# The eight scatter steps of an expert pair, three of them between the parts of the lin product or all behind it

## The chip, the cores and the metric

One core of a Trainium2 chip runs the whole kernel in one launch. The metric is the device time of one execution in microseconds (us); three executions of the kernel before are given, and one more that was taken by the hardware profiler. Five engines work side by side, each with its own queue: TensorE (PE; its weight loads are listed apart as PEld), VectorE (DVE), ScalarE (ACT), GpSimd (POOL) and SyncE (SP), which issues most transfers.

## The reference

Two layers over 512 latent tokens of 1024 values: a token mixer (a gated DeltaNet in layer 0, a short gated convolution in layer 1), then in each layer a hierarchical mixture of 32 SwiGLU experts, of which each token uses two. The change lies in the mixture, of which this is the core:

```python
def expert_block(args):
    xi, e = args
    return (jax.nn.silu(xi @ w1[e]) * (xi @ w3[e])) @ w2[e]

yb = lax.map(expert_block, (xb, block_e)).reshape(cap, d)
y = jax.ops.segment_sum(yb * buf_w[:, None].astype(yb.dtype), buf_tok, num_segments=t + 1)
```

Each token's row is gathered, goes through its expert, is weighted, and is added back to the token it came from. All values are float32; w1 and w3 of one expert are 1024 x 512 and w2 is 512 x 1024, 2 MiB each.

## The kernel before, in words

The mixture of a layer is `moe(l)` (L1454 and on). It takes the 32 experts two at a time, 16 pairs `p`, each expert with up to 64 rows, so that a pair fills 128 rows: the first 64 columns of the array hold one expert's rows and the last 64 the other's. If an expert of a pair has more than 64 rows, a second block of 128 rows (tiles `hx`, `gx`) goes through the same weights, under checks of the count `n` (`tc.If(n > 64)`, L1626, L1633 and L1642).

The order of the work in a pair is the order of the program text, as the stage is scheduled by hand:

- `gate_up` (L1499): the w1 product. `up` (L1493) runs over k = 0..7 and over the two experts x, 16 matmuls (32 records, as each float32 matmul leaves two); ScalarE takes silu of the result.
- `lin_up` (L1502): the w3 product in the same way; VectorE multiplies it into `g`. I call it the lin product or the w3 product.
- a scatter of the previous pair's result: eight steps (`scatter_parts`, L1550 to L1559), each of two matmuls of a selection matrix with the high and the low part of the result (L1556, L1557), into one of the PSUM banks `pj`, and one add of that bank to the residual `xs` on VectorE (L1558). There are six `pj` banks (`self.banks = {"tr": 2, "pj": 6}`, L434).
- `turn_g` (L1508, L1510) transposes `g`, `turn` (L1479, L1483, L1485) transposes and modulates the rows `hg` of the next pair to `hT`, half on VectorE and half on ScalarE.
- `down` (L1520 and on): the w2 product in two halves, weighed on VectorE (L1526) and split into a high and a low part on ScalarE (L1530) and GpSimd (L1531).

`up` takes a generator `side` and, after the k of a list, lets it do one step. That is how work is put between the parts of a product:

```python
for _ in range(side[1].count(k) if side else 0):
    next(side[0], None)
```

In the kernel before, the lin product of pairs 1 to 14 gets the scatter with the list (1, 3, 5): a step after k = 1, 3 and 5. The other five follow behind the product, after the check for the second block, the gather for pair p + 2 (GpSimd) and `issue` (SyncE).

The weights come through three rings of 2 MiB slots, 3 + 2 + 4 = 9. `next_unit` takes the next weight, `issue` starts the next transfers in a fixed order (w1, w3, w2 of a pair, two transfers each) as slots come free; a transfer waits on SyncE until the slot's last reader on TensorE is done. The pair 15 of a layer is written apart, with a scatter of its own, and pair 0 has no scatter.

Of the kernel before, what the change touches and what calls it, by code (L numbers as in the profile page):

```python
# [34 lines left out]
class Net:  # L35
# [83 lines left out]
    def plan(self):  # L119
# [18 lines left out]
        def moe(l):  # L138
            for p in range(16):
                for n in ("w1", "w3", "w2"):  # L140
                    order.extend((n, l, 2 * p + x) for x in range(2))
        moe(0)
        for g in range(2):
            order.extend(("w_in_b", 3072, u + g, 0) for u in (0, 2, 4))
            if g == 0:
                order.extend(("ada_w", 6144, 4 * b + u, l) for l, b in self.later for u in range(4))
        order.extend(("w_out_b", 1024, u, 0) for u in range(2))
        moe(1)

        self.place = {o: "B" for o in order if o[0] in ("ada_w", "w_in_b") or o[:2] == ("w2", 0) and o[2] > 29}  # L150
# [1303 lines left out]
    def moe(self, l):  # L1454
        tc, nc, I = self.tc, self.nc, self.I
        with ExitStack() as ms:
# [7 lines left out]
            def gather(gi, hg=None, skip=False, of=None):  # L1464

                if hg is None:
                    hg = wk.tile([128, 1024], F32, name="hg", bufs=2)
                of = self.hscr if of is None else of
                nc.gpsimd.indirect_dma_start(out=hg, out_offset=None, in_=of[:, :],
                                             in_offset=bass.IndirectOffsetOnAxis(ap=gi, axis=0),  # L1470
                                             **(dict(bounds_check=of.shape[0] - 1, oob_is_err=False) if skip else {}))
                return hg

            def turn(hg, to=None):

                hT = (wk.tile([128, 1024], F32, name="hT") if to is None else to).rearrange("p (k d) -> p k d", k=8)
                ps = [self.bank("tr") for _ in range(2)]
                for c in range(8):
                    nc.tensor.transpose(ps[c // 4][:, 128 * (c % 4):128 * (c % 4) + 128], hg[:, c::8], self.ident)  # L1479
                for c in range(8):  # L1480
                    q = ps[c // 4][:, 128 * (c % 4):128 * (c % 4) + 128]
                    if c > 3:
                        nc.scalar.activation(hT[:, c], q, AF.Identity, bias=self.m8[:, l, 2, c:c + 1], scale=self.m8[:, l, 0, c:c + 1])  # L1483
                    else:
                        nc.vector.tensor_scalar(hT[:, c], q, self.m8[:, l, 0, c:c + 1], self.m8[:, l, 2, c:c + 1], op0=OP.mult, op1=OP.add)  # L1485
                return hT

            def up(hT, w, side=()):

                ps = self.bank("pj")  # L1490
                for k in range(8):
                    for x in range(2):
                        nc.tensor.matmul(ps[64 * x:64 * x + 64], hT[:, k, 64 * x:64 * x + 64], w[x][:, k], start=(k == 0), stop=(k == 7))  # L1493
                    for _ in range(side[1].count(k) if side else 0):
                        next(side[0], None)
                return ps

            def gate_up(hT, w, g, side=()):
                nc.scalar.activation(g, up(hT, w, side), AF.Silu)  # L1499

            def lin_up(hT, w, g, side=()):
                nc.vector.tensor_tensor(g, up(hT, w, side), g, op=OP.mult)  # L1502

            def turn_g(g, gT=None):

                pg = self.bank("tr")
                for k in range(4):
                    nc.tensor.transpose(pg[:, 128 * k:128 * k + 128], g[:, k::4], self.ident)  # L1508
                gT = wk.tile([128, 4, 128], F32, name="gT") if gT is None else gT[:, :512].rearrange("p (k d) -> p k d", k=4)
                nc.scalar.activation(gT, pg.rearrange("p (k d) -> p k d", k=4), AF.Copy)  # L1510
                return gT

            def down(gT, w, ti, wi, o, y, eng=nc.gpsimd):

                self.sel(o, ti)
                for n in range(2):
                    py = self.bank("pj")
                    for k in range(4):
                        for x in range(2):
                            nc.tensor.matmul(py[64 * x:64 * x + 64], gT[:, k, 64 * x:64 * x + 64], w[x][:, k, 512 * n:512 * n + 512],  # L1520
                                             start=(k == 0), stop=(k == 3))
                    weigh(py, n, wi, y)
                    split(n, o, y, eng)
# [17 lines left out]
            def ident(x1):  # L1541
                for t in range(4):
                    nc.tensor.matmul(x1[t], self.ident, self.xs[:, t, 512:], start=True, stop=False)
                    yield

            def scatter(*a):
                for _ in scatter_parts(*a):
                    pass

            def scatter_parts(yhi, ylo, sel, ns=(0, 1)):  # L1550
                for n in ns:
                    for t in range(4):
                        ps = self.bank("pj")
                        c = slice(512 * n, 512 * n + 512)
                        s = sel[:, 128 * t:128 * t + 128]
                        nc.tensor.matmul(ps, s, yhi[:, c], start=True, stop=False)  # L1556
                        nc.tensor.matmul(ps, s, ylo[:, c], start=False, stop=True)  # L1557
                        nc.vector.tensor_tensor(self.xs[:, t, c], ps, self.xs[:, t, c], op=OP.add)  # L1558
                        yield n, t  # L1559

            def col(t, c):
                return t[:, c:c + 1]
# [3 lines left out]
            def out():  # L1566
                return tuple(wk.tile([128, m], F32R, name=n) for n, m in (("yhi", 1024), ("ylo", 1024), ("sel", 512)))
# [5 lines left out]
            def more(p):  # L1573
                n = count(slice(p, p + 1))
                with tc.If(n > 64):
                    gather(col(self.gxc, 16 + p), hx[p % 2])
                return n
# [37 lines left out]
            hT = turn(hgs.pop(0))  # L1615
# [4 lines left out]
            prev = None  # L1620
            for p in range(15):
                n = ns.pop(p)
                w = self.next_unit(), self.next_unit(1)
                g = wk.tile([128, 512], F32, name="g")
                gate_up(hT, w, g, () if p else (route, range(8)))
                with tc.If(n > 64):  # L1626

                    hTx = turn(hx[p % 2], hx[p % 2])
                    gate_up(hTx, w, gx)
                w = self.next_unit(), self.next_unit(1)  # L1630
                add = scatter_parts(*prev) if prev else iter(())
                lin_up(hT, w, g, (add, (1, 3, 5)))
                with tc.If(n > 64):  # L1633
                    lin_up(hTx, w, gx)
                if p < 14:
                    hgs.append(gather(col(self.gix, p + 2), skip=True))
                    self.issue(self.taken)
                for _ in add:
                    pass
                w = self.next_unit(), self.next_unit(1)  # L1640
                prev = out()
                with tc.If(n > 64):  # L1642
                    down(turn_g(gx, hx[p % 2]), w, col(self.tid, 16 + p), col(self.wsl, 16 + p), prev, gx)
                    scatter(*prev)
                gT = turn_g(g)
                hT = turn(hgs.pop(0))
                if p < 13:
                    ns[p + 2] = more(p + 2)
                prev = out()
                down(gT, w, col(self.tid, p), col(self.wsl, p), prev, g, nc.gpsimd if p < 14 else nc.vector)  # L1650

            n = count(slice(15, 16))
            w = self.next_unit(), self.next_unit(1)
            g = wk.tile([128, 512], F32, name="g")
            add = scatter_parts(*prev, ns=(1, 0))
            gate_up(hT, w, g, (add, (2, 3, 3, 4, 5, 6, 7)))
            w = self.next_unit(), self.next_unit(1)
            x1 = [self.bank("pj") for _ in range(4)]
            add = chain(add, ident(x1))
# [17 lines left out]
            prev = out()  # L1677
# [252 lines left out]
```

## Time and profile before

| what | us |
|---|---|
| median of three executions | 1875.29 |
| lowest and highest | 1871.93, 1875.86 |
| the profiled execution, its own time | 1876.28 |
| span of the profiled execution | 1874.2 |
| layer 0's expert pairs, first w1 product to the last pair's | 622.6 to 1088.1 |
| layer 1's expert pairs, the same | 1363.3 to 1822.1 |

The span runs from the first to the last instruction; the execution's time has 2.1 us around it. TensorE is busy 91% of the span, and its granted clock is 0.964 of full speed in the mean. The transfers move 572 MB, 305 GB/s over the whole span. The shares are means over stages with different limits: what a saved microsecond is worth is read from the two expert stages themselves.

### The profile page before, as it was taken

Reading aid. Unit: us, or ns where it says so; the run is one execution under the profiler, and the core shown is the slowest. Engines: PE = TensorE matmul, PEld = TensorE weight load, DVE = VectorE, ACT = ScalarE, POOL = GpSimd, SP = SyncE. Lnnn points to the kernel's source line nnn. Section 1 sums busy time; section 2 is a strip of 40 time slices with the busy share of each in tenths; the row PEclk is TensorE's granted clock in tenths of the full one; section 3 lists DMA queues with packets and bytes.
Section 4 is the critical chain, followed back from the end, with each engine's and each line's share of the span. In section 5 each row is a group of like instructions: output and inputs, shape, how many; then the busy total and the mean of one; then the engine's idle time right before and its main releaser. Section 6 shows DMA issues by size and latency. Waiting matters only on the chain. (4 is left out here: it accounts for less than half of the span.)

```text
span 1874.2 us, 26554 instructions
## 1 busy us (share of the span) xinstructions
PE 1709.8 (91%) x10229; PEld 977.8 (52%) x10230; DVE 814.8 (43%) x1611; ACT 483.3 (26%) x888; POOL 415.4 (22%) x297
## 2 busy tenths in 40 slices
PE   5999988997988799999999988999799999999997
PEld 4766667776866344434434336688534344344332
DVE  5435877746664332323323237633523233233233
ACT  4465354523223111111111115223211111111112
POOL 1114464635410101111010103343111111110100
PEclk9999989998998899999999998999899999999998
DMA  9569975779835899999998953714589969999993
GB/s 330 192 241 339 293 222 157 173 170 262 244 107 227 345 425 425 427 425 426 426 425 346 404 193 139 279 40 180 226 340 427 425 268 425 426 425 425 426 418 123
DMA packets 154551, 572.33 MB, mean 305 GB/s; under 512 B 55208, under 2 KB 79961, under 8 KB 126214
## 3 DMA queue, kind: packets, MB, share of 16 engines
q1 hardware_dynamic: 148326, 555.26, 77.6%
q0 software_dynamic: 4896, 10.48, 1.5%
q10 hardware_dynamic: 1152, 4.19, 0.5%
q8 instruction: 115, 1.88, 0.4%
q14 instruction: 62, 0.51, 0.1%
HBM read 550.86 MB, written 26.38 MB: 308 GB/s over the span
## 5 line engine op out<-in xcount | busy, mean ns | idle before, releaser
L1493 PE MATMUL pj<-w,hT 128*64 128x512 f32 x2048 | 482.7, 602 | 7.1 <-DMA w<-in_w 2.5
L1558 DVE TENSOR_TENSOR xs<-pj,xs 128x512 f32<-128x512 f32 x264 | 170.5, 687 | 372.9 <-PE pj L1557 369.1
L1493 PEld LDWEIGHTS pj<-w,hT 128*64 128x64 f32 x2048 | 151.4, 137 | 266.1 <-issue 251.3
L1531 POOL TENSOR_TENSOR ylo<-g,yhi 128x512 fp32r<-128x512 f32 x56 | 70.8, 1265 | 653.4 <-ACT yhi L1530 653.4
L1520 PE MATMUL pj<-w,gT 128*64 128x512 f32 x960 | 212.6, 594 | 3.0 <-DVE hT L1485 1.6
L666 POOL TENSOR_TENSOR wlo<-w,whi 128x1024 fp32r<-128x1024 f32 x43 | 106.5, 2479 | 230.2 <-ACT whi L664 228.7
L1520 PEld LDWEIGHTS pj<-w,gT 128*64 128x64 f32 x960 | 78.1, 137 | 116.5 <-issue 108.8
L1526 DVE SCALAR_TENSOR_TENSOR g<-pj,wsl,gate 128x512 f32<-128x512 f32 x64 | 48.0, 751 | 177.7 <-PE pj L1520 164.1
L1556 PE MATMUL pj<-yhi,sel 128*128 128x512 f32 x264 | 117.5, 445 | 4.9 <-PEq L1633 4.2
L1510 ACT ACTIVATE gT<-tr 128x512 f32<-128x512 f32 x32 | 19.1, 598 | 383.5 <-PE tr L1508 383.5
L1556 PEld LDWEIGHTS pj<-yhi,sel 128*128 128x128 f32 x264 | 49.4, 187 | 120.0 <-issue 90.4
L681 PE MATMUL pj<-w,whi 128*128 128x512 f32 x336 | 105.7, 394 | 0.6 <-ACT whi L664 0.6
L1557 PE MATMUL pj<-ylo,sel 128*128 128x512 f32 x264 | 104.3, 395 | 1.3 <-POOL ylo L1531 1.3
L681 PE MATMUL pj<-hhi,wlo 128*128 128x512 f32 x224 | 93.7, 419 | 8.3 <-POOL wlo L666 7.0
L681 PE MATMUL pj<-hhi,whi 128*128 128x512 f32 x224 | 93.4, 417 | 6.4 <-DVE cv L797 5.5
L681 PE MATMUL pj<-hlo,whi 128*128 128x512 f32 x224 | 91.5, 409 | 0.0
L1530 ACT ACTIVATE yhi<-g 128x512 fp32r<-128x512 f32 x62 | 39.2, 632 | 193.3 <-DVE g L1526 193.3
L681 PEld LDWEIGHTS pj<-w,whi 128*128 128x128 f32 x336 | 63.7, 190 | 15.2 <-ACT whi L664 1.0
L664 ACT ACTIVATE whi<-w 128x1024 fp32r<-128x1024 f32 x53 | 55.3, 1054 | 53.9 <-PE pj L681 37.6
L1499 ACT ACTIVATE g<-pj 128x512 f32<-128x512 f32 x32 | 19.1, 598 | 190.5 <-PEq L1626 141.1
L681 PE MATMUL pj<-w,wlo 128*128 128x512 f32 x168 | 66.3, 394 | 0.0
L1483 ACT ACTIVATE hT<-tr,m 128x128 f32<-128x128 f32 x128 | 48.3, 458 | 55.2 <-PE tr L1479 53.5
(613 smaller groups left out, 2692.1 us busy)
## 6 DMA issues: line engine op xcount, KB each, us to landing
w<-in_w SPq DMA_DIRECT2D x188, 2048.0 KB
w<-in_ada_w SPq DMA_DIRECT2D x20, 2048.0 KB
w<-in_w_in_a SPq DMA_DIRECT2D x8, 2048.0 KB
w<-in_w_in_b SPq DMA_DIRECT2D x6, 2048.0 KB
w<-in_ada_w SPq DMA_DIRECT2D x8, 1024.0 KB
w<-in_w SPq DMA_DIRECT2D x8, 1024.0 KB
Y<-R SPq DMA_DIRECT2D x20, 256.0 KB
vp<-vscr SPq DMA_DIRECT2D x18, 256.0 KB
```

Of the source, the lines that this page charges most:

```text
L664: nc.scalar.activation(hi[:, :, :n], w, AF.Copy)
L666: (lo_eng or nc.gpsimd).tensor_tensor(lo[:, :, :n], w, hi[:, :, :n].bitcast(F32), op=OP.subtract)
L681: nc.tensor.matmul(out, n[j][0][:, k], n[j][1][:, k, a:b], start=(i == 0), stop=(i == 23))
L1483: nc.scalar.activation(hT[:, c], q, AF.Identity, bias=self.m8[:, l, 2, c:c + 1], scale=self.m8[:, l, 0, c:c + 1])
L1493: nc.tensor.matmul(ps[64 * x:64 * x + 64], hT[:, k, 64 * x:64 * x + 64], w[x][:, k], start=(k == 0), stop=(k == 7))
L1520: nc.tensor.matmul(py[64 * x:64 * x + 64], gT[:, k, 64 * x:64 * x + 64], w[x][:, k, 512 * n:512 * n + 512], start=(k == 0), stop=(k == 3))
L1526: nc.vector.scalar_tensor_tensor(y, py, wi, self.gate[:, 512 * n:512 * n + 512], op0=OP.mult, op1=OP.mult)
L1530: nc.scalar.activation(o[0][:, c], y, AF.Copy)
L1531: eng.tensor_tensor(o[1][:, c], y, o[0][:, c].bitcast(F32), op=OP.subtract)
L1556: nc.tensor.matmul(ps, s, yhi[:, c], start=True, stop=False)
L1557: nc.tensor.matmul(ps, s, ylo[:, c], start=False, stop=True)
L1558: nc.vector.tensor_tensor(self.xs[:, t, c], ps, self.xs[:, t, c], op=OP.add)
```

## The change

The lin product of pairs 1 to 14 gets no `side` any more, and all eight scatter steps stand where the last five stood.

```diff
                 w = self.next_unit(), self.next_unit(1)
-                add = scatter_parts(*prev) if prev else iter(())
-                lin_up(hT, w, g, (add, (1, 3, 5)))
+                lin_up(hT, w, g)
                 with tc.If(n > 64):
                     lin_up(hTx, w, gx)
                 if p < 14:
                     hgs.append(gather(col(self.gix, p + 2), skip=True))
                     self.issue(self.taken)
-                for _ in add:
-                    pass
+                if prev:
+                    scatter(*prev)
                 w = self.next_unit(), self.next_unit(1)
```

The lines behind it move up by one (L1633 is L1632 in the changed kernel, L1642 is L1641). The first place is TensorE's queue in a pair of layer 0, from the check behind the w1 product; `hx_5990` is the second block's tile, which is passed over when no expert of the pair has more than 64 rows. Before:

```order
L1493 MATMUL pj<-w,hT 64x512 x4
L1556 MATMUL pj<-yhi,sel 128x512
L1557 MATMUL pj<-ylo,sel 128x512
L1493 MATMUL pj<-w,hT 64x512 x4
L1556 MATMUL pj<-yhi,sel 128x512
L1557 MATMUL pj<-ylo,sel 128x512
L1493 MATMUL pj<-w,hT 64x512 x4
L1556 MATMUL pj<-yhi,sel 128x512
L1557 MATMUL pj<-ylo,sel 128x512
L1493 MATMUL pj<-w,hT 64x512 x4
L1633 COMPARE_AND_BRANCH
```

With the change:

```order
L1493 MATMUL pj<-w,hT 64x512 x16
L1632 COMPARE_AND_BRANCH
L1493 MATMUL pj<-w,hx_5990 64x512 x16
L1632 UNCONDITIONAL_BRANCH x2
L1556 MATMUL pj<-yhi,sel 128x512
L1557 MATMUL pj<-ylo,sel 128x512
L1556 MATMUL pj<-yhi,sel 128x512
L1557 MATMUL pj<-ylo,sel 128x512
```

The product's 16 matmuls stand without a break, and behind the check come eight steps (four of their rows are shown), where five stood.

The second place is VectorE's queue at the same point, up to the next pair's `hT` (the branch at L1642 goes past the second block's work). Before:

```order
L1558 TENSOR_TENSOR xs<-pj,xs 128x512 x3
L1502 TENSOR_TENSOR g<-pj,g 128x512
L1633 COMPARE_AND_BRANCH
L1502 TENSOR_TENSOR gx<-pj,gx 128x512
L1633 UNCONDITIONAL_BRANCH x2
L1558 TENSOR_TENSOR xs<-pj,xs 128x512 x5
L1642 COMPARE_AND_BRANCH
```

With the change:

```order
L1502 TENSOR_TENSOR g<-pj,g 128x512
L1632 COMPARE_AND_BRANCH
L1502 TENSOR_TENSOR gx<-pj,gx 128x512
L1632 UNCONDITIONAL_BRANCH x2
L1558 TENSOR_TENSOR xs<-pj,xs 128x512 x8
L1641 COMPARE_AND_BRANCH
```

The three adds that stood ahead of the product's own multiplication (L1502) stand behind it, in a row of eight, ahead of the branch and of `hT`.

The third place is TensorE's queue behind the row of eight, from the branch past the second block to the w2 product, with the semaphores that each waits for (`DVE_49` is VectorE's count); these rows read the same before, but for the line of the branch:

```order
L1641 UNCONDITIONAL_BRANCH [waits PE_49]
L1508 MATMUL tr<-ident,g 128x128 x4
L1479 MATMUL tr<-ident,hg 128x128 [waits DMASW4_49,PE_49,Activation_49]
L1479 MATMUL tr<-ident,hg 128x128 x3
L1479 MATMUL tr<-ident,hg 128x128 [waits Activation_49]
L1479 MATMUL tr<-ident,hg 128x128 x3
L1570 TENSOR_LOAD cnt_5976
L1575 COMPARE_AND_BRANCH
L1575 UNCONDITIONAL_BRANCH x2
L1520 MATMUL pj<-w,gT 64x512 [waits DMAHW4_49,DVE_49]
```

The transposes wait for ScalarE and for the gathered rows; the w2 product's first matmul waits for its weight and for VectorE's count, which by its place in the program stands behind the eight adds and the branch, not behind `hT`.

## Rows read from the trace of the kernel before

**Rows 1.** The page: busy us of the engines, share of the span, instructions.
```profile
PE 1709.8 (91%) x10229; PEld 977.8 (52%) x10230; DVE 814.8 (43%) x1611; ACT 483.3 (26%) x888; POOL 415.4 (22%) x297
```

**Rows 2.** Stretches: us, engines' busy us, granted clock, DMA share, GB/s; two answers.
```profile
636.10:951.60 315.50, 303.03 (x1348) 128.23 (x1344) 95.07 (x168) 43.67 (x88) 39.82 (x34) 1.00 1.01 425
...
1003.00:1031.00 28.00, 26.33 (x124) 12.93 (x122) 12.88 (x23) 4.61 (x9) 3.81 (x3) 1.00 0.68 289
...
1511.00:1535.80 24.80, 23.14 (x110) 12.08 (x110) 12.87 (x23) 4.61 (x9) 3.81 (x3) 1.00 0.44 171
...
1536.80:1800.80 264.00, 256.95 (x1146) 106.20 (x1142) 82.01 (x144) 36.37 (x74) 33.08 (x28) 1.00 1.01 425
...
1376.80:1494.80 118.00, 113.78 (x518) 47.45 (x516) 32.66 (x60) 17.39 (x36) 15.08 (x13) 1.00 1.01 423
```

**Rows 3.** Timeline of TensorE, pair 4 of layer 0: start us, us, instruction.
```profile
738.60 7.09 PE L1493 MATMUL pj<-w,hT 128*64 128x512 f32 x32
...
745.84 1.94 PE L1493 MATMUL pj<-w,hT 128*64 128x512 f32 x8
...
755.53 0.47 PE L1556 MATMUL pj<-yhi,sel 128*128 128x512 f32 x1 [0.16 <-PEq L1633]
...
756.07 0.40 PE L1556 MATMUL pj<-yhi,sel 128*128 128x512 f32 x1
...
757.45 0.39 PE L1556 MATMUL pj<-yhi,sel 128*128 128x512 f32 x1
...
758.21 0.72 PE L1508 MATMUL tr<-ident,g 128*128 128x128 f32 x4
...
760.54 7.09 PE L1520 MATMUL pj<-w,gT 128*64 128x512 f32 x32 [0.20 <-DVE hT L1485]
...
767.42 1.06 PE L1493 MATMUL pj<-w,hT 128*64 128x512 f32 x4
```

**Rows 4.** Timeline of TensorE, layer 0: pair 11, start of pair 12.
```profile
940.62 7.36 PE L1493 MATMUL pj<-w,hT 128*64 128x512 f32 x32
...
948.12 1.04 PE L1493 MATMUL pj<-w,hT 128*64 128x512 f32 x2
...
951.62 3.08 PE L1493 MATMUL pj<-w,hT 128*64 128x512 f32 x6 [2.46 <-DMA w<-in_w]
...
974.68 7.07 PE L1493 MATMUL pj<-w,hT 128*64 128x512 f32 x32
```

**Rows 5.** Waits of TensorE over the whole span: us in total, times, longest.
```profile
PE pj L1493 <- DMA w<-in_w: 2.5, 1, 2.5
```

**Rows 6.** Instructions on tile hx, TensorE: duration in ns, first and last start.
```profile
L1493 PE MATMUL pj<-w,hx x128: 592/592/643, 983.3 to 1510.6; 128*64 128x512 f32 x128
```

**Rows 7.** Timeline of VectorE, pair 4 of layer 0.
```profile
748.48 0.69 DVE L1558 TENSOR_TENSOR xs<-pj,xs 128x512 f32<-128x512 f32 x1 [8.79 <-PE pj L1557]
...
756.33 3.08 DVE L1558 TENSOR_TENSOR xs<-pj,xs 128x512 f32<-128x512 f32 x5
...
759.57 1.37 DVE L1485 TENSOR_SCALAR hT<-tr,m 128x128 f32<-128x128 f32 x4 [0.15 <-DVEq L1642]
...
760.84 0.48 DVE L1698 TENSOR_SCALAR sel<-tok,tid 128x512 fp32r<-128x512 f32 x1
```

**Rows 8.** Timeline: issues of SyncE, and TensorE at layer 1's pair 14.
```profile
635.12 0.82 SPq L215 DMA_DIRECT2D w<-in_w  x2
...
1375.82 0.81 SPq L215 DMA_DIRECT2D w<-in_w  x2
...
1535.82 17.48 SPq L215 DMA_DIRECT2D w<-in_w  x6
...
1800.78 0.65 PE L1493 MATMUL pj<-w,hT 128*64 128x512 f32 x2 [0.16 <-PEq L1626]
```

**Rows 9.** DMA queues: packets, MB, share of 16 engines.
```profile
q0 software_dynamic: 4896, 10.48, 1.5%
```

**Rows 10.** The stretch behind the wait of pair 11, columns as in rows 2.
```profile
951.60:956.00 4.40, 4.38 (x10) 1.27 (x12) 0.13 (x1) 0.00 (x0) 0.00 (x0) 0.61 1.01 419
```

## The prediction

> **What bounds the kernel now.** I read the page first, then the busy time in stretches of the two expert stages, then one pair of experts on TensorE and VectorE, then the few waits on weights. The page has TensorE busy for 1709.8 of 1874.2 us [rows 1]: it is the engine to look at, but not proof that it sets the end, so the transfers have to be laid beside it. From 636.1 to 951.6 us in layer 0, and from 1536.8 to 1800.8 us in layer 1, the DMA share is full (1.01) at 425 GB/s; but one stretch behind the first (1003 to 1031) and one ahead of the second (1511 to 1535.8) have shares of 0.68 and 0.44: there the transfers stood still for want of a free slot [rows 2]. So there are two regimes, and which one a pair is in decides whether TensorE's time counts.
>
> How fast is each? TensorE takes 28.82 us from one pair's w1 product (738.60) to the next (767.42) [rows 3]. The transfers: the first stretch runs from the second w3 transfer of pair 1, issued at 635.12 [rows 8], to the landing of the second w3 of pair 11, which is 61 transfers of 2 MiB in 315.5 us, 5.17 us each and 31.0 us for the six of a pair. TensorE is faster than the transfers by 2.2 us a pair and lives on a lead: nine slots that were filled ahead. In layer 0 the lead runs out at pair 11: its w3 product, begun at 948.12, stands still for 2.46 us for a weight and goes on at 951.62 [rows 4]; that is the one such wait, 2.5 us, of the whole run [rows 5]. Pair 12 is one with more than 64 rows: its second block of rows (tile hx, from 983.3 on) uses weights that are there already, while the transfers run ahead and stop. Such a pair comes once a layer, since 128 records are four up products, two blocks of two [rows 6]; in layer 1 it is pair 4.
>
> **The change, part by part.** In a pair (1 to 14 of each layer) the w3 product had three scatter steps between its parts; now it has none, and all eight steps follow it.
>
> What is removed from the product: with three steps inside, it takes 745.84 to 755.53, 9.69 us. The w1 product, 32 records of the same kind without a break, takes 738.60 to 745.84, 7.24 us, the check behind it included [rows 3]. The product's own cost is taken as the same, so 2.45 us go, 0.82 for each step.
>
> What is added behind it: in the row of five steps that stands there now, the second begins at 756.07 and the fifth at 757.45, 0.46 us apart [rows 3]. Three more are 1.38 us. So TensorE gains 2.45 - 1.38 = 1.07 us a pair: a step costs 0.82 between column halves and 0.46 among its own kind.
>
> What is moved on VectorE: its three adds of 0.69 us each lay in idle time inside the product [rows 7]; now eight stand in a row. In the row of five they take 3.08 us, 0.62 each, slower than TensorE's 0.46, and begin 0.80 us after the row's first matmul (756.33 after 755.53). Eight end at 0.80 + 8 x 0.62 = 5.8 us. Behind them in VectorE's queue stand the first half of the next pair's hT (759.57, 0.15 us behind the last add) and sel [rows 7]. Who waits for that? The down product waits for VectorE's count behind the adds; TensorE comes to it 760.54 - 755.53 = 5.01 us after the row's start [rows 3], with three more steps at 6.4. The adds are over at 5.8, plus 0.15 for the branch: some 0.45 us to spare. hT is needed only at the next w1 product, 6.9 us later. The seventh and eighth step take over the banks of the first and second (six pj banks, of which the w1 and w3 products have let go): they are issued at 2.8 and 3.2 us, those adds end at 1.4 and 2.0. So VectorE's new tail is costed at nothing, under TensorE's row; if that cover went, its price is that of the second rival. The transfer issues and the gather of the same pair keep their order in the queues of SyncE and GpSimd, and the two issues that wait for the w3 product's end come 2.45 us earlier. They add nothing, as more are waiting in a full queue.
>
> What this is worth, stage by stage. In layer 0 pairs 1 to 10 gain nothing: whatever TensorE saves, the second w3 of pair 11 still lands at 951.6, because the queue was full from 636.1 on [rows 2]. From that landing on, nothing waits for a weight [rows 5], so the w3 product of pair 11 and those of 12, 13 and 14 gain in full: 4 x 1.07 = 4.3 us. In layer 1 pairs 1 to 4 run on a lead, as no wait for a weight stands there at all [rows 5]: another 4.3 us. Their lead carries it: from 1376.8, behind the issue of the second w3 of pair 1 at 1375.82 [rows 8], to pair 4's w3 product 118 us later, 423 GB/s moved 49.9 MB [rows 2], and the 19 transfers needed by then are 39.8 MB. At 1535.82, with the extra block done, the transfers start afresh when TensorE frees a slot [rows 8], so they shift with it and the 4.3 us are kept. From there they run full again, and what TensorE can gain is the lead that is left at pair 14, its last w3 product behind them, begun at 1800.78 [rows 8]. In these 264.0 us, 425 GB/s are 112.2 MB; needed by then are 51 transfers, 106.9 MB, and some 3 MB of gathered rows (10.48 MB for 34 gathers in the whole run [rows 9]). The surplus of 2.3 MB is 5.4 us. But the first stretch shows by how much such a count is ahead of the landing: 134.1 MB by the count against 127.9 + 3 MB needed, a good 7 us in 315.5, or 6 us in 264. So the lead at pair 14 lies between 0 (TensorE did not wait there) and 5.4 us; I take 1 us, near the lower end, for the reason of the first stretch. Behind it pair 14's own row gains its 1.07 us.
>
> The sum: 4.3 + 4.3 + 1.0 + 1.1 = 10.7 us. The profiled execution took 1876.28 us, 2.1 more than its span; that becomes 1865.6. The median of the runs shown, 1875.29, lies 1.0 us under the profiled one, so the predicted median is 1864.6 us. With the bounds of the lead, 0 and 5.4 us, it is 1865.6 and 1860.2.
>
> **A price from a page, weighed.** The row shows 425 GB/s in both stretches [rows 2]. The Trainium skill, "DMA: Bandwidth & Descriptors", Specifications, gives some 358 GB/s per core as what the HBM lets through. By that a pair's 12.9 MB would take an estimated 36 us, every pair would wait for weights, and the change would be worth nothing. The row says otherwise, and the sum goes by the row.
>
> **The rivals.** First: no change. The transfers set the end of both stages and every microsecond saved is waited for again. For it: full DMA share in 580 us of the two stages. Against it: the two stretches at 0.68 and 0.44, where the transfers waited for TensorE. It gives 1875.3 us. The 358 GB/s of the Trainium skill, weighed above, are this rival's rule.
>
> Second, on the other side: the row goes at VectorE's pace. If TensorE had to wait for a bank at each step, the row would take 0.80 + 8 x 0.62 + 0.38 = 6.1 us up to the transposes instead of 8 x 0.46 + 0.38 = 4.1, and a pair would be 1.0 us slower than now. It decides from the point where fewer banks are free than adds are outstanding: at the eighth step VectorE has done (3.2 - 0.8) / 0.62, nearly 4, so 4 are outstanding and 4 banks would be too few; six are there. The price: 14 pairs in layer 1, 14.0 us, and 14 in layer 0, of which the 5.2 us that pair 11 lost (34.06 us from 940.62 to 974.68 [rows 4], against 28.82) come back: 22.8 us, 1898 us. Against it: in the row of five TensorE kept its 0.46 although the adds went at 0.62. The Trainium skill, in "Trainium Kernel Development and Optimization", Best Practices, warns that tiling TensorE speeds up the compute and not the emptying of PSUM, which is this rival's rule; the row of five does not bear it out.
>
> Third: TensorE's whole saving counts, as earlier frees let the transfers go faster: 28 x 1.07 = 30.0 us, 1845 us. For it: TensorE's 91% and a single wait. Against it: 31.0 us a pair at full DMA share, against 27.75 us that TensorE would then take.
>
> Fourth, a smaller gain: the clock. In the 4.4 us behind the 2.46 us stall the granted clock was 0.61 in the mean [rows 10], so it lay at the lower of the two levels for most of them; 0.39 of 4.4 us is 1.7 us lost to TensorE. With the change the lead is used up at 31.0 - 27.75 = 3.25 us a pair: what lasted 10 pairs at 2.2 us in layer 0 lasts nearly 7, and in layer 1 some 1 + 8 x 2.2 us at pair 6 last 6. So stalls of some 3 us in a pair come from pair 7 or 8 on, and in layer 1 from 12 on. In pairs that wait anyway this is hidden; at pair 14 of layer 1 it isn't. Then it is 1866.3 us.
>
> **How the numbers follow.** A measurement of this kernel tells some 0.2%, 3.8 us, from no change. The forecast, with the lead's bounds, has 0.56; the clock or another small loss (a gain of 4 to 9 us) 0.24; no change 0.10; all of TensorE's saving 0.04; slower 0.06. The range reaches from 1858, below the lead's upper bound by a run's scatter of 2 us, to 1871 us, a gain of 4: it leaves out the last three cases, 2 in 10. Faster by over 0.2%: 0.56 + 0.24 + 0.04 = 0.84; within: 0.10; slower: 0.06.
>
> **What would show it.** Right: the w3 product takes 7.2 us in one run of 32 records; eight steps 0.46 us apart; the down product 6.4 us after the row's start; a pair of 27.7 us where no weight is waited for; waits on w in layer 0 from pair 7 or 8 on, some 3 us a pair, and in layer 1 from 12 on; the stretch behind 951.6 shorter by 4.3 us. Wrong: steps 0.62 us apart, or the down product later than 6.6 us after the row's start (VectorE's tail is not covered); w waits in layer 1 before pair 11 (the lead was smaller); no w waits at all (the transfers went faster); or the 4.3 us of layer 0 given back in the mixer between the stages.

## The result, and the profile after

The change takes 1865.45 us (median of 5 runs, 1861.91 to 1865.52) against 1874.16 for the kernel before on the same chip: a ratio of 0.9948 with a 95% interval of 0.9934 to 0.9963, or 7 to 12 us less. The profiled execution took 1864.34 us, its span is 1862.3.

The page has TensorE busy for 1692.0 us, 17.8 less than [rows 1]; the span fell by 11.9. The new row of a pair stands in TensorE's timeline, pair 4 of layer 0 (start us, us, engine, line, operation, tiles, shape, records, and the idle time ahead with what ended it):

```profile
740.23 7.09 PE L1493 MATMUL pj<-w,hT 128*64 128x512 f32 x32 [0.16 <-PEq L1626]
...
751.51 0.72 PE L1508 MATMUL tr<-ident,g 128*128 128x128 f32 x4
...
753.83 7.09 PE L1520 MATMUL pj<-w,gT 128*64 128x512 f32 x32 [0.20 <-DVE hT L1485]
```

The w3 product is one run of 32 records, 740.23 to 747.47 where the first of eight scatter steps begins; it took 9.69 us in [rows 3] and takes 7.24. The steps begin at 747.47, 748.01, 748.47 and so on to 750.74, 0.46 us apart. From one w1 product to the next (733.03 to 760.72) a pair takes 27.69 us, before 28.82. VectorE, same pair:

```profile
748.27 4.87 DVE L1558 TENSOR_TENSOR xs<-pj,xs 128x512 f32<-128x512 f32 x8
753.29 1.37 DVE L1485 TENSOR_SCALAR hT<-tr,m 128x128 f32<-128x128 f32 x4 [0.15 <-DVEq L1641]
```

The eight adds end at 753.14, `hT` begins 0.15 us later, and the w2 product 0.54 us after that. Behind the transposes (751.51) it begins 2.32 us later, as in [rows 3] (758.21 to 760.54): VectorE's longer tail holds nobody up. The bracket of the w2 row names `hT` as what ended its wait in both traces, and the idle time there is 0.20 us in both; which of VectorE's instructions the count stands for, the trace does not tell.

What the pairs wait for, in the stretch of layer 0's pairs and then of layer 1's (TensorE's waits: us in total, times, longest):

```profile
PE pj L1493 <- DMA w<-in_w: 8.3, 5, 2.5
...
PE pj L1493 <- DMA w<-in_w: 4.4, 2, 2.8
```

Before there was one such wait [rows 5]. Now the w3 products of pairs 7 to 11 of layer 0 wait, and these pairs last 29.8, 30.4, 30.6, 30.1 and 33.9 us instead of 27.7; so do pairs 12 and 13 of layer 1 (30.2 and 34.2). TensorE, layer 1's pair 13 and the start of 14:

```profile
1748.81 7.07 PE L1493 MATMUL pj<-w,hT 128*64 128x512 f32 x32
1756.02 1.04 PE L1493 MATMUL pj<-w,hT 128*64 128x512 f32 x2
1759.89 9.96 PE L1493 MATMUL pj<-w,hT 128*64 128x512 f32 x30 [2.83 <-DMA w<-in_w]
1783.03 7.04 PE L1493 MATMUL pj<-w,hT 128*64 128x512 f32 x32
```

Where the 11.9 us of the span come from, by the starts of the w1 products in both timelines (us):

| stretch | before | after | gain |
|---|---|---|---|
| ahead of the experts of layer 0 | 622.58 | 619.75 | 2.83 |
| layer 0, pair 0 to the start of pair 15 | 465.54 | 461.38 | 4.16 |
| pair 15 and the mixer of layer 1 | 275.17 | 276.39 | -1.22 |
| layer 1, pairs 0 to 3 | 115.98 | 112.68 | 3.30 |
| layer 1, pair 4 with its second block | 56.36 | 55.26 | 1.10 |
| layer 1, pairs 5 to 13 | 257.96 | 257.57 | 0.39 |
| layer 1, pair 14 | 28.53 | 27.42 | 1.11 |
| pair 15 and the end | 52.08 | 51.85 | 0.23 |

The stretches with the change in them gain 10.1 us. The first row is scatter: up to there the program is the same, and over the ten profiled executions in which it is (the two above and eight of the experiments) layer 0's pair 0 starts between 618.8 and 624.5 us. So profiles are compared by stretch below, not by span.

### The profile page after: what moved, and what is told of

Same layout as the page of the kernel before. It is cut to its first block, busy times and chain, and to the rows that moved or that the text cites. A ratio compares the mean times of both kernels' runs of the same rounds, so it can differ in the third digit from the quotient of the medians.

```text
span 1862.3 us, 26581 instructions
## 1 busy us (share of the span) xinstructions
PE 1692.0 (91%) x10229; PEld 1002.6 (54%) x10230; DVE 808.3 (43%) x1611; ACT 482.4 (26%) x888; POOL 414.9 (22%) x297
## 5 line engine op out<-in xcount | busy, mean ns | idle before, releaser
L1493 PE MATMUL pj<-w,hT 128*64 128x512 f32 x2048 | 474.2, 602 | 17.5 <-DMA w<-in_w 12.8
L1493 PEld LDWEIGHTS pj<-w,hT 128*64 128x64 f32 x2048 | 167.7, 138 | 295.5 <-issue 262.5
L1502 DVE TENSOR_TENSOR g<-pj,g 128x512 f32<-128x512 f32 x32 | 22.1, 692 | 429.0 <-PEq L1632 386.7
L1558 DVE TENSOR_TENSOR xs<-pj,xs 128x512 f32<-128x512 f32 x264 | 162.5, 681 | 19.2 <-PE pj L1557 15.5
L1556 PE MATMUL pj<-yhi,sel 128*128 128x512 f32 x264 | 108.0, 409 | 4.6 <-DVE g L1526 0.4
```

## The experiments

The theory: a step costs 0.46 us among its own kind and 0.36 more where it breaks a product; the change takes three breaks from every pair, and the saving counts where transfers do not set the pace: pairs 11 to 14 of layer 0, pairs 1 to 4 and 14 of layer 1, and about 1 us of lead in pairs 5 to 13 there. Rivals: all 28 pairs count, or others do; the steps, not the breaks, cost the time; the transfers do not limit.

**The change in the pairs called hidden, and in the others.** Two kernels: the old list where `p` is not in `BARE`, the new order where it is. The first has the pairs below in `BARE`, the second pairs 11 to 14 of layer 0 and 1 to 4 and 14 of layer 1.

```diff
+BARE = {0: range(1, 11), 1: range(5, 14)}
-                lin_up(hT, w, g, (add, (1, 3, 5)))
+                at = () if p in BARE[l] else (1, 3, 5)
+                lin_up(hT, w, g, (add, at))
```

> The change in 19 pairs alone: 1 to 10 of layer 0 and 5 to 13 of layer 1, the pairs that in my reading run against the transfers. My theory: TensorE's 1.07 us of each of them is waited for again at the next weight, so 0 to 1 us in all (the lead left at pair 14 of layer 1), ratio to the kernel before 0.9995 to 1.000. Rival, every pair counts alike: 19 of 28 parts of the 8.7 us measured, 5.9 us, ratio 0.997. Rival, TensorE alone sets the end: 19 x 1.07 = 20 us, ratio 0.989.

> The change in the other 9 pairs alone: 11 to 14 of layer 0, 1 to 4 and 14 of layer 1. My theory: they carry the whole gain, 9 x 1.07 = 9.6 us, ratio to the kernel before 0.995, as the full change. Rival, every pair counts alike: 9 of 28 parts of 8.7 us, 2.8 us, ratio 0.9985.

Measured: 19 hidden pairs give 0.9995 (0.9984 to 1.0006), 1873.0 us against 1875.0; the 9 open ones 0.9956 (0.9941 to 0.9972), 1865.6 us. So nine pairs carry what the change brings, within the interval. By their profiled executions, both layers' pairs 0 to 14 together take 924.4 us before, 922.0 with the change in the hidden pairs and 913.4 with it in the open ones: 2.4 and 11.0 us less, of which 1.7 each come from the clock in pair 11 of layer 0 (table below). The waits on weights of TensorE, of the first and of the second kernel:

```profile
PE pj L1496 <- DMA w<-in_w: 10.2, 6, 2.9
```
```profile
PE pj L1496 <- DMA w<-in_w: 2.5, 1, 2.5
```

In the hidden pairs the time that TensorE saved came back at the weights: there are five more waits, and the w3 product of layer 0's pair 11 goes on behind its weight 329.17 us after the start of pair 0, against 329.05 before.

**Half of the w2 transfers left out, with and without the change.** In pairs 0 to 14 the second w2 of a pair is not moved and the first one's slot is used in its place; the rest of the program is untouched.

```diff
+            if o[0] == "w2" and o[2] % 2 and o[2] < 30:
+                self.issued.append(self.same)
+                continue
...
+            self.same = self.issued[-1]
```

> The kernel before without every second w2 transfer of pairs 0 to 14 (the second expert of a pair uses the first one's w2), so that a pair moves 5 transfers of 2 MiB in place of 6, some 26 us at 5.17 us each, under TensorE's 28.8. My theory: no wait for a weight is left in either layer, and some 5 to 8 us go (the 5.2 us that pair 11 of layer 0 lost, and its clock). If the transfers never bounded a pair, the time stays within 2 us of the kernel before.

> The changed kernel with the same transfers left out (the second expert of a pair uses the first one's w2), 26 us of transfers a pair against TensorE's 27.75. My theory: now every one of the 28 pairs gains, 28 x 1.07 = 30 us against the run before this one that has the same transfers left out; pairs last 27.7 us throughout. Rival, something else than the transfers took two thirds of the gain (VectorE's tail, the clock, a cost given back later): the difference stays at about 9 us.

Measured: 0.9953 (0.9939 to 0.9967), 1865.78 us, without the change, and 0.9779 (0.9763 to 0.9796), 1832.9 us, with it: the change is worth 32.9 us where the transfers are lighter, nearly four times as much as with all of them, and near the 30.0 of all 28 pairs. Neither trace has a wait on w in a w3 product. Between their two profiled executions the pairs of layer 0 gain 13.7 us and those of layer 1 15.4, close to 14 x 1.07 = 15.0 each. So the transfers are what takes the rest of TensorE's saving. The kernel without the change gained some 10 us instead of 5 to 8: 6.2 lie in layer 0's pairs (pair 11 without its wait, at full clock), 4.3 between the stages, of which 2.4 are a shorter wait in pair 15 (below).

**Three steps at one place of the product**, in every pair, five behind it as before.

```diff
-                lin_up(hT, w, g, (add, (1, 3, 5)))
+                lin_up(hT, w, g, (add, (3, 3, 3)))
```

> The kernel before with its three steps inside the w3 product at one place, all behind k = 3, in place of one behind each of k = 1, 3 and 5. If what costs is the change between column halves and the full array (0.36 us at each of three places), two of the three go: the product takes 7.24 + 0.36 + 3 x 0.46 = 9.0 us in place of 9.69, a pair gains 0.72 us, the 9 open pairs 6.5 us, ratio 0.9965. If what costs is the step itself wherever it stands in the product (a wait for its bank or its own weights, 0.82 each), the product stays at 9.7 us and the ratio at 1.000.

Measured: 0.9942 (0.9926 to 0.9958), 1863.52 us. TensorE, pair 4 of layer 0:

```profile
746.44 3.65 PE L1493 MATMUL pj<-w,hT 128*64 128x512 f32 x16 [0.15 <-PEq L1626]
750.02 0.50 PE L1556 MATMUL pj<-yhi,sel 128*128 128x512 f32 x1
...
751.60 3.65 PE L1493 MATMUL pj<-w,hT 128*64 128x512 f32 x16
755.42 0.47 PE L1556 MATMUL pj<-yhi,sel 128*128 128x512 f32 x1 [0.16 <-PEq L1633]
```

746.44 to 755.42 are 8.98 us: 7.24 + 3 x 0.46 + 0.36. Three steps and one break cost what the theory says, and the pair (739.20 to 767.34) takes 28.14 us, 0.68 under [rows 3]. That is 60% of the change's 1.13 (two thirds were expected); but the whole kernel came out as fast as the change. So it was run once more, beside the change itself:

> The change itself once more, on one chip with the next run. Both theories: a ratio of 0.995, some 10 us less than before.

> Three steps at one place of the product once more, now beside the change itself. A step in a row costs 0.46 us and a break 0.36 us, so one break instead of three is worth two thirds of the change: 6.7 us less than before, 0.9965, and some 3 us more than the change. Rival: the number of breaks does not matter from one on, and it is as fast as the change (0.995) or faster, as the first look had it.

Measured: the change 0.9941 (0.9925 to 0.9958), 1863.79 us; one break 0.9944 (0.9927 to 0.9962), 1865.53 us. The order is now as the theory has it, but 1.7 us, like the 1.9 the other way between the first runs, which were not beside each other, are less than the intervals' halves of some 3 us: by their times the two are not told apart. By stretches they are. From the start of pair 0 to that of pair 15, both layers added, the change's two profiled executions need 914.3 and 913.0 us, those of one break 915.5 and 915.7, before 924.4. One break gains 8.8 of the change's 10.1 to 11.3, and not two thirds. Two things were left out of its expectation. The lead of layer 1's pairs 5 to 13 is worth the same about 1 us to either (one break gains 1.1 there, 257.96 to 256.88). And in layer 0 the lower clock behind the wait in pair 11 costs 1.7 us that count in full, where it falls there, as it does in the profiled execution of the kernel before. In both runs of one break it fell in pair 10 instead (from 921.5 and 920.3 on, against 952.3), where the wait for the next weights hides it. Layer 0, cut at the moment at which the w3 product of pair 11 goes on behind its wait, shows both effects apart (us; the granted clock in the 5 us behind that moment, as a share of full speed):

| kernel | start of pair 0 to that moment | from there to the start of pair 15 | granted clock |
|---|---|---|---|
| before | 329.05 | 136.50 | 0.50 for 3.4 us of it |
| the change | 329.12 | 132.25 | 0.50 for 3.4 us of it |
| the change, second time | 330.15 | 130.57 | 1.00 |
| hidden pairs alone | 329.17 | 134.82 | 1.00 |
| open pairs alone | 329.43 | 130.64 | 1.00 |
| one break, twice | 329.12, 329.37 | 132.17, 132.08 | 1.00 |

The rows of the change, the hidden and the open pairs at that moment:

```profile
948.88 8.78 PE L1493 MATMUL pj<-w,hT 128*64 128x512 f32 x30 [2.48 <-DMA w<-in_w]
...
947.96 1.93 PE L1496 MATMUL pj<-w,hT 128*64 128x512 f32 x6 [1.09 <-DMA w<-in_w]
...
950.48 7.08 PE L1496 MATMUL pj<-w,hT 128*64 128x512 f32 x30 [2.48 <-DMA w<-in_w]
```

With the hidden pairs alone, pairs 11 to 14 are those of the kernel before; 134.82 against 136.50 is thus the price of the lower clock, 1.7 us. At either clock the change is worth 4.2 us in these four pairs (136.50 to 132.25, and 134.82 to 130.6; 4 x 1.07 = 4.3), and one break 2.7 (4 x 0.68). So where a saving counts, one break gives the 60 to 65% that a pair's own timeline shows, and the 8.8 us of the whole are nine pairs' 6.1, the lead's 1.1 and the clock's 1.7.

**What a break is made of.** In two kernels the old order is kept, and a step is one float32 matmul of the high part alone (the low part is left out): once on the whole array, as the scatter is, and once in two column halves, as the products are. This tells whether leaving the product costs, or changing the form of the array.

```diff
-                        nc.tensor.matmul(ps, s, yhi[:, c], start=True, stop=False)
-                        nc.tensor.matmul(ps, s, ylo[:, c], start=False, stop=True)
+                        for x in range(2):
+                            o = slice(64 * x, 64 * x + 64)
+                            nc.tensor.matmul(ps[o], s[:, o].bitcast(F32), yhi[:, c].bitcast(F32), start=True, stop=True)
```

(the other: one such line with `ps` and `s` whole)

> The kernel before with other scatter steps: float32 matmuls in two column halves, like the expert products, of the high part alone (the low part of the result is left out). A step in a row should take 0.86 us, as a pair of column-half matmuls of the products does. If the change between column halves and the full array is what a break costs, there is none here: three steps inside the w3 product take 0.86 each, and the product 7.24 + 2.6 = 9.8 us. If any break costs 0.36, whatever the form: 10.9 us.

> The same with float32 matmuls over the full array (the high part alone; the low part is left out): a step in a row 0.86 us. If the change of the array's form costs, three steps inside the product take 0.86 + 0.36 = 1.22 each and the product 10.9 us. If it was the change between float32 and the scatter's other number format that cost, there is none here and the product takes 9.8 us, as in the run with column halves.

TensorE, pair 4 of layer 0, in halves:

```profile
750.48 1.94 PE L1493 MATMUL pj<-w,hT 128*64 128x512 f32 x8
752.22 1.06 PE L1558 MATMUL pj<-yhi,sel 128*64 128x512 f32 x4
753.07 1.92 PE L1493 MATMUL pj<-w,hT 128*64 128x512 f32 x8
...
760.29 4.51 PE L1558 MATMUL pj<-yhi,sel 128*64 128x512 f32 x20
```

and on the whole array:

```profile
751.58 1.94 PE L1493 MATMUL pj<-w,hT 128*64 128x512 f32 x8
753.45 1.13 PE L1556 MATMUL pj<-yhi,sel 128*128 128x512 f32 x2
754.50 1.94 PE L1493 MATMUL pj<-w,hT 128*64 128x512 f32 x8
...
762.45 4.53 PE L1556 MATMUL pj<-yhi,sel 128*128 128x512 f32 x10 [0.16 <-PEq L1632]
```

In halves the product takes 750.48 to 760.29, 9.81 us, which is 7.24 + 3 x 0.86: a step inside costs no more than in a row. On the whole array it takes 751.58 to 762.45, 10.87 us, with the five steps behind it as long (4.51 and 4.53 us): 1.06 more for three breaks, 0.35 each. So it is the change between column halves (128*64) and the whole array (128*128), there and back, that costs, not leaving the product. Nor is it the number format, as all these matmuls are float32 in both kernels. The Trainium skill, "TensorEngine Tiling (Array Packing)", Key Properties, says that a switch of the tiling mode, unlike one of the tile, drains TensorE; the traces agree in that such a switch costs, 0.35 us for the way there and back, but a drain as such is not to be seen in them. As a whole the kernels take 1933.73 and 1966.76 us (one run each): a float32 step costs 0.86 where two float32r matmuls cost 0.46.

**The same in pair 15.** It is written apart: seven steps stand in its w1 product, the eighth and two of four identity products (`ident`, on the whole array) in its w3 product. All go into rows, the steps behind the w1 product, the identity products behind the w3 product:

```diff
-            gate_up(hT, w, g, (add, (2, 3, 3, 4, 5, 6, 7)))
+            gate_up(hT, w, g)
+            for _ in add:
+                pass
...
-            add = chain(add, ident(x1))
-            lin_up(hT, w, g, (add, (0, 1, 2)))
-            for _ in add:
+            lin_up(hT, w, g)
+            for _ in ident(x1):
                 pass
```

> The changed kernel, and in pair 15 of each layer too the w1 product without scatter steps inside (eight steps at seven breaks before; now in a row between w1 and w3 product) and the w3 product without the three identity products inside (all four behind it). Pair 15 waits for no weight in either layer, so my theory counts it in full: 7 x 0.36 = 2.5 us for the scatter and some 3 x 0.2 us for the identity products (1.05 us inside against 0.86 in a row), 3.1 us a layer, 6.2 us on top of the change: some 15 us under the kernel before, ratio 0.992. Rival: VectorE's adds, the banks or w2's late transfer take the place of what goes: ratio 0.995, as the change alone.

Measured: 0.9883 (0.9866 to 0.9899), 1852.89 us: 21.8 us less than before, where 15 were expected. From pair 15's w1 product to its transposes of `g` layer 1 needs 21.40 us instead of 24.23: 2.83 us for eight breaks fewer (nine become one), 0.35 each. The expectation had 3.1 us; it counted three identity products inside the w3 product, where two stand, and priced them apart. The rest lies behind: a branch past the work for longer blocks, then the w2 product. TensorE and VectorE there, in the change, layer 0 and then layer 1 (the view of the first row ends inside the w2 product, after 28 of its 32 records; the whole takes 10.05 us):

```profile
1111.18 9.19 PE L1538 MATMUL pj<-w,gT 128*64 128x512 f32 x28 [5.19 <-PEq L1664]
...
1103.75 0.69 DVE L1502 TENSOR_TENSOR g<-pj,g 128x512 f32<-128x512 f32 x1 [7.99 <-PE pj L1493]
1110.86 0.48 DVE L1697 TENSOR_SCALAR sel<-tok,tid 128x512 fp32r<-128x512 f32 x1 [6.42 <-PEq L1664]
...
1838.04 8.44 PE L1538 MATMUL pj<-w,gT 128*64 128x512 f32 x32 [2.73 <-PEq L1664]
...
1833.05 0.69 DVE L1502 TENSOR_TENSOR g<-pj,g 128x512 f32<-128x512 f32 x1 [7.97 <-PE pj L1493]
1837.72 0.49 DVE L1697 TENSOR_SCALAR sel<-tok,tid 128x512 fp32r<-128x512 f32 x1 [3.98 <-PEq L1664]
```

and in this kernel:

```profile
1108.69 8.78 PE L1538 MATMUL pj<-w,gT 128*64 128x512 f32 x32 [3.53 <-PEq L1665]
...
1108.37 0.48 DVE L1698 TENSOR_SCALAR sel<-tok,tid 128x512 fp32r<-128x512 f32 x1 [6.47 <-PEq L1665]
...
1828.06 7.09 PE L1538 MATMUL pj<-w,gT 128*64 128x512 f32 x32 [0.69 <-ACTq L1665]
...
1827.68 0.49 DVE L1698 TENSOR_SCALAR sel<-tok,tid 128x512 fp32r<-128x512 f32 x1 [3.60 <-PEq L1665]
```

TensorE waits 1.7 us less in layer 0 and 2.0 in layer 1; but from the end of `g` (L1502) to `sel` behind the branch VectorE waits the same in both, 6.4 and 6.5 us in layer 0, 4.0 and 3.6 in layer 1. So a new theory: the way past the branch takes a time of its own, counted from the end of `g`, and TensorE's work behind the w3 product covers a part of it, four identity products now instead of two. The rival: the w1 product's new order shortens the wait. Two kernels, each with one half of the edit:

> The change, and in pair 15 the w3 product without its three breaks, the eighth scatter step ahead of it and the four identity products in a row behind it; the w1 product keeps its steps. If TensorE's wait behind the branch to the last pair's w2 product counts from the end of g (3.8 us in layer 1, 6.4 in layer 0) and work behind the w3 product covers it: 3 breaks of 0.36 us and 1.8 us of cover in each layer, 5.8 us less than the change, ratio 0.992; TensorE's wait behind the branch 0.9 us at most in layer 1 and 3.5 in layer 0. Rival: the wait got shorter by the w1 product's new order; then it stays at 2.6 and 5.2 us, and 2.2 us are gained over the change.

> The change, and in pair 15 the w1 product without steps, the eight steps behind it; in the w3 product stand three identity products and only the fourth behind it. By the cover theory the wait behind the branch grows by the 0.9 us of the identity product that stood behind, to 3.6 us in layer 1 and 6.1 in layer 0, and of the five breaks' 1.8 us a layer 0.9 is left: 1.8 us less than the change in all. Rival (the w1 product's order sets the wait): the wait falls to 0.7 and 3.5 us, and 7 us are gained over the change.

The w2 products of the first (w3 part alone), and then of the second (w1 part alone):

```profile
1107.08 8.78 PE L1538 MATMUL pj<-w,gT 128*64 128x512 f32 x32 [3.46 <-PEq L1665]
...
1828.43 7.09 PE L1538 MATMUL pj<-w,gT 128*64 128x512 f32 x32 [0.69 <-ACTq L1665]
```
```profile
1112.89 8.81 PE L1538 MATMUL pj<-w,gT 128*64 128x512 f32 x32 [5.94 <-PEq L1666]
...
1835.88 8.78 PE L1538 MATMUL pj<-w,gT 128*64 128x512 f32 x32 [3.39 <-PEq L1666]
```

The w3 part alone has the short waits, the w1 part alone waits longer than the change: the cover theory stands, the rival falls. Up to the transposes of `g` the two halves save 1.05 us for three breaks and 1.80 for five. The w3 part alone is 0.9882 (0.9863 to 0.9902), 1853.03 us, 10.8 less than the change in the same comparison, where 5.8 were expected; the other took 1862.50 us in its one run, where the change's runs go from 1861.25 to 1866.58. Of the 8.1 us between the profiled spans of the w3 part and of the change, 2.86 lie from pair 15 of layer 0 to the start of layer 1's pairs, as expected, and 4.39 in layer 1's pair 15: 2.9 as expected, and 1.4 in the w2 product, which takes 8.50 us in the change and 7.09 here, as the clock fell to half at the end of the change's 2.62 us wait and did not fall in the 0.69. The remaining 2.7 us between the medians I did not trace; they are within the intervals. Both kernels with rows in pair 15 beat the change and the kernel before; which of the two is faster the runs do not tell.

## Why the prediction was right, point by point

- **The sum, 10.7 us**: 8.7 us between the medians, 10.7 in the second comparison, 10.1 and 11.3 by the stretches of the two profiled executions; 1.7 of the 11.3 are the clock in pair 11, which stayed up in the second.
- **The w3 product, 9.69 to 7.24 us, and the row, 0.46 us a step**: both as predicted to the hundredth. 0.82 against 0.46 was read from the old trace; the cause, which the prediction left open beyond "between column halves", is the change of form (0.35 us).
- **VectorE's tail at nothing**: right. The adds were said to end 5.8 us after the row's start, to leave some 0.45 us; they end 5.67 after it (747.47 to 753.14), `hT` starts 0.15 later and the w2 product 6.36 after the row's start (predicted 6.4).
- **Layer 0, pairs 11 to 14 alone, 4.3 us**: 4.25 from the moment at which pair 11's product goes on (951.62 to 1088.12 before, 948.88 to 1081.13 now), and nothing up to it (329.05 and 329.12). The hidden pairs by themselves gave nothing there, and in the whole run nothing outside the interval.
- **Layer 1, pairs 1 to 4, 4.3 us**: 3.30 + 1.10 = 4.4.
- **Layer 1, pairs 5 to 13, 1.0 us of a possible 5.4, and pair 14, 1.07**: 0.39 and 1.11. Together, from pair 5 to pair 15's start, 286.49 us became 284.99, a gain of 1.5; in the change's second profiled execution and the three of pair 15's kernels, which have the same pairs, it is 284.48, 284.44, 284.33 and 284.22, a gain of 2.0 to 2.3 where 2.1 was predicted. So the choice near the lower end was right, and that the lead is used up; the 1 us itself was chosen between the bounds, not worked out. The count of bytes would have given 5.4. Its terms were rough: the queue of the gathered rows moved 3.7 MB in the first stretch and 1.9 in the second, not some 3 in each, and when the 61st transfer had landed at 951.6, the weights' queue had moved 129.8 MB, 1.9 more than the 127.9 of the 61. It is the landing, not the bytes moved, that has to be read.
- **Waits from pair 7 on, and from 12 on in layer 1**: seven waits, in just these pairs (in the second execution pairs 8 to 11, and 12 to 14). Their records are 1.0 to 2.8 us; the pairs last 2.1 to 3.0 us longer than 27.7, or 6.2 and 6.5 where the clock fell too, where some 3 were expected.
- **The stretches between and behind**, costed at nothing: -1.22 and 0.23 us, and 0.57 and 0.30 in the second execution: no loss that both show.
- **The first rival, no change**, falls with the whole result and with the lighter transfers. **The second, at VectorE's pace**, falls with the 0.46 us between steps. **The third, all of 30 us**, is what the change gives once the transfers are lighter (32.9): its mechanism is real, and the condition that the prediction put against it (31.0 us a pair of transfers) is what decides. **The fourth, the clock**, came half true: in pair 13 of layer 1 the granted clock is at the lower level for 6.8 us, from the last microsecond of a wait on, as a stretch of it shows (columns as in [rows 2]):

```profile
1759.00:1765.60 6.60, 5.71 (x14) 1.72 (x16) 0.00 (x0) 0.00 (x0) 0.00 (x0) 0.50 1.00 422
```

  The fall makes pair 13 longer (34.2 us; 31.4 in the change's second execution, where the clock stayed up), but there pair 14 waits in its place (29.5 us against 27.4): of the 2.9 us by which pair 13 is longer, the two stretches above keep 0.5.

## What to carry to other kernels

Put matmuls that use the whole array in a row of their own, and not between those of a column-tiled product: every way there and back costs about 0.35 us here, whatever the step is worth by itself. Before counting what that saves, find the pairs in which the saving is not waited for again: nine of 28 gave nearly all of it here. And where a queue has to pass a branch, put independent work right ahead of it, behind what the branch has to wait for.

## What the hardware showed beyond that

- The way past the taken branch of pair 15 takes 3.6 to 4.1 us from the end of `g` to `sel` where the transfers are nearly quiet, and 6.4 to 6.5 where they are full. The busy time of the two stretches in the change (us from and to, length, the engines' busy us, granted clock, DMA share, GB/s):

```profile
1104.44:1110.86 6.42, 1.55 (x7) 0.83 (x5) 0.00 (x1) 2.29 (x4) 0.00 (x0) 0.96 1.05 386
1833.74:1837.72 3.98, 1.58 (x7) 0.83 (x5) 0.01 (x1) 2.08 (x3) 0.00 (x0) 0.96 0.03 6
```

  With half of the w2 transfers left out, layer 0's was 4.0 us without the change and 3.8 with it, at shares of 0.25 and 0.28. The Trainium skill, "Runtime: NRT & Kernel Launch", Instruction fetch mechanics, says that a taken branch out of the window at hand has its target fetched by DMA before anything goes on. The traces agree: on each of these ways the DMA queue q8, of the kind "instruction", moves one packet of 16 KB, and `sel` begins a fixed time behind that packet's end. By the start of the packet, its length and the time from its end to `sel` (us):

| way | end of `g` to the packet | the packet | its end to `sel` |
|---|---|---|---|
| the change, layer 0 | 3.79 | 1.11 | 1.52 |
| the change, layer 1 | 1.08 | 1.36 | 1.53 |
| rows in pair 15, layer 0 | 3.82 | 1.12 | 1.53 |
| rows in pair 15, layer 1 | 1.11 | 0.96 | 1.52 |
| the change with fewer transfers, layer 0 | 1.11 | 1.17 | 1.50 |

  In all fourteen traces (before, change and the experiments), two ways each, the last column lies between 1.49 and 1.61 us. So the 2.4 us between a quiet and a full way come from a later start of the packet: some 1.1 us behind the end of `g` (once 1.6), or 3.8. That the packet starts later because of the other transfers is borne out by the two runs with fewer of them; what holds it back in detail, no run shows.
- A wait costs more than its length where the clock falls in it or right behind it. In layer 1's pair 15 the same w2 product took 7.09 us behind a wait of 0.69 us and 8.44 to 8.78 behind waits of 2.6 to 3.4 in the change (twice) and in the w1 part alone. It does not always fall: with the change in the nine open pairs alone, the product took 7.09 us behind 2.62.
